# One gate's products moved beside the last delta-rule inverse, with split pools and new durations in the planner

## The chip, the cores and the metric

The kernel runs on one core of a Trainium2 chip. The metric is the device time of one execution in microseconds (us), median of several runs. TensorE (PE) multiplies matrices into PSUM, VectorE (DVE) and ScalarE (ACT) do elementwise work and empty PSUM, GpSimd (POOL) does elementwise work that needs no PSUM, and SyncE (SP) issues nearly all DMAs, in one queue in order.

## The reference

One layer of a hybrid streaming encoder on a sequence of 1024 frames of width 1024, in float32. Cut to what matters here:

```python
h = rmsnorm(x); proj = h @ w_in                     # gdn q,k,v,z,..., gla q,k,v,r,..., gate_a, gate_b
o_a = gated_delta_rule_chunked(q_a, k_a, v_a, ...)  # 8 heads; a unit-triangular solve per chunk, then a scan
o_b = gla_chunked(...)                              # 4 heads
y_a = (rmsnorm(o_a) * silu(z)) @ w_branch_gdn
y_b = (rmsnorm(o_b) * silu(r)) @ w_branch_gla
x = x + (sigmoid(gate_a) * y_a + sigmoid(gate_b) * y_b) @ w_out
x = x + cross_attention(rmsnorm(x), rmsnorm(mem))
x = x + relu(rmsnorm(x) @ w1) ** 2 @ w2
return rmsnorm(x)
```

## The kernel before

**Products.** A float32 operand is split into a high part (`hi`, ACT rounds it, L584) and a rest (`lo`, `raw - hi` on DVE or POOL, L585), and a product is three matmuls of 128x128 by 128x512: hi by hi (L544), hi by lo (L546), lo by hi (L548). Such matmuls are called dense here. Projections use a Strassen-like scheme (`wino`, `gla_dense`) or the plain one (`g_fm`: 2 halves x 8 blocks x 3 = 48 dense matmuls).

**Stages.** `phase0` (norms and memory keys), `phase_gla`, `phase_gdn` (the delta rule), then the merge, the output projection, attention and the MLP. `phase_gdn` works through four pairs of heads. For a pair it makes k, q and v with a convolution (`push_conv`), solves the triangular systems in two parts (a 32-step substitution on DVE and POOL in `gdn_subst`, then `gdn_inverse`), and runs the scan over 8 chunks (`gdn_scan`). The operands of the next pair's convolutions are pushed as generators; `fill(n)` takes n dense matmuls from them, so that dense work is written between the small steps.

**The inverse.** `gdn_inverse` combines 32x32 inverses into 64x64 and 128x128 ones. Per head it has four groups of small matmuls, each needing PSUM results of the one before, copied by ACT or DVE: L1394 (copied at L1395 and L1396), L1403 (copied at L1404 and L1407), L1410 (copied at L1412), L1417 (copied at L1418). Then the scan may begin (L1452). Between the groups stands `fill(nfill)`, with nfill = `GF[6]` = 8.

**The last pair.** Here there is no next pair. The products of gate 5 (`push_gate`: tile `tg`, stored by DMA at L1521) are pushed behind the last convolutions, and before the last inverse

```python
                else:
                    self.drain()
                    ectx.close()
                    wctx.close()
                    ob = self.begin_merge()
```

runs all of them, closes the pools of the stage (`pge`, and `w1` of the weights) and opens those of the merge. `begin_merge` queues the first merge weights (`raw` from `in_w_bgla_dram`) and loads the operands of the first five merge products through staging tiles `e` (from `obd`) into the slots B0a, B0b, A1a, A1b and A0a. The merge's first products (`yb`) multiply weights in tiles `wop` by B0a.

**Order.** The program is traced once, then `Plan` makes an order for each engine: it simulates all instructions with durations from `Op.__init__`, picks by latest start, chooses DVE or POOL for additions that both can do (`flex`), and the order found is fixed with dependencies. Engines take their instructions strictly in that order. A pool may only be written once the instructions on tiles that lay there before are done, and the planner keeps a load behind the closing of every pool that it overlaps. So which matmul stands next to which is set by these costs, pools and the order of the text.

Of the kernel before, what the change touches and what calls it, by code (L numbers as in the profile page):

```python
# [45 lines left out]
LOV = (0, 2, 5)  # L46
GLG, GN = 0, (0, 0, 0, 1)
ZA = "z"
# [34 lines left out]
class Op:  # L83
# [5 lines left out]
    def __init__(self, ins, flex):  # L89
# [27 lines left out]
        if scan:  # L117
            vec = 65 + wide * 2.08
        elif ins.opcode == "StreamTranspose":
            vec = (830 if rough else 90) + wide * 1.042  # L120
        elif ins.opcode == "Reciprocal" or n <= 16 and wide <= 16:
            vec = 82
        pool = {"Memset": 20 + n * 0.875, "TensorScalarAffineSelect": 140 + n * 0.89, "TensorCopy": 140 + n * 0.9}
        self.costs = costs = {"vector": vec, "gpsimd": 245 + n * 1.98 if sums else pool.get(ins.opcode, 100 + n)}
        if sums and n <= 16:
            costs["gpsimd"] = 330 + 160 * n
        if ins.opcode == "DMACopy":
            self.dma, self.cost, self.lat = True, 60, 2600
            self.bytes = n * 4 * outs[0].ap[0][1]
        elif eng == "tensor":  # L130
            m = size(ins_[0])
            if ins.is_transpose:
                self.cost = m * 0.85
            elif ins_[0].dtype == F32R:
                self.cost = m * 0.4427 + (4 if m < HALF else 0)
            else:
                self.cost = max(m, size(ins_[1])) * 1.667 + 8
            self.lat = 205
        elif eng == "scalar":
            self.cost = (60 if psum(ins_[0]) else 95) + n * (1.71 if rough else 0.834) + 90 * min(cols, 1) + 90 * (len(outs) > 1)  # L140
            self.lat, self.own = 140, 130
        else:
            self.port = eng == "gpsimd" or two
            self.place(eng)
# [321 lines left out]
class Layer:  # L466
# [152 lines left out]
    def slot(self, name, shape=(NB, HALF), dt=F32R):  # L619

        pool = self.bp if name[0] == "A" else self.bp2 if name[1] == "0" else self.bp3
        return self.til(pool, (P,) + shape, name, dt, bufs=1)
# [533 lines left out]
    def phase_gla(self):  # L1156
        nc, a = self.nc, self.a
        with ExitStack() as ctx:
# [31 lines left out]
            for h in range(LH):  # L1190
# [32 lines left out]
                if h < LH - 2:  # L1223
                    self.push_gates(sp, 5 + h)
                if h == LH - 2:
                    for i in range(5, 5 + GLG):
                        self.push_gate(i, lambda src: self.wpart(src, [NB, P], nc.vector), sp, "ex", EXB, T)
                self.fill(FG if h == 1 else FE)
# [296 lines left out]
    def phase_gdn(self, wctx):  # L1525

        nc, a = self.nc, self.a
        with ExitStack() as lctx:
            ectx, sctx = ExitStack(), ExitStack()
            sv = self.pool(lctx, "pgv", "left", bufs=2)  # L1530
# [4 lines left out]
            for tag in ("k1", "kdt1", "NT1", "q"):  # L1535
                self.til(sq, [P, T], tag, bufs=2)
            for tag in ("k0", "kdt0", "NT0", "dm", "acc"):
                self.til(sp, [P, T], tag, bufs=2)
            self.til(sq, [P, T], "X", bufs=2)
            self.subTA = self.til(sq, [P, 16, 64], "subTA", bufs=1)  # L1540
# [4 lines left out]
            def push_keys(hs):  # L1545
                par = hs[0] // 2 % 2
                sts = [{"pool": sq if par else sp, "tag": lambda t: f"{t}{par}"} for _ in hs]
                for h, st in zip(hs, sts):
                    st["k"] = self.til(st["pool"], [P, NB, P], st["tag"]("k"), bufs=2)
                    conv(f"k{h}", GH + h, a["w_gdn"][3 * h], lambda acc, st=st: st["k"])  # L1550
                return sts
# [8 lines left out]

            gates = iter(range(5 + GLG, 6))
            getw = lambda src: self.wpart(src, [NB, P])
            last = None
# [3 lines left out]
            for p in range(GH // 2):  # L1567
# [10 lines left out]
                if p < GH // 2 - 1:  # L1578
                    nxt = push_keys((2 * p + 2, 2 * p + 3))
                for _ in range(GN[p]):  # L1580
                    self.push_gate(next(gates), getw, sp)
                if last:
# [12 lines left out]
                self.gdn_queries(sv, sp, sts[1])  # L1595
                self.until(f"v{hs[1]}")
                self.gdn_v(sv, sts[0])
                self.fill(GF[4])
                self.gdn_v(sv, sts[1])
                self.fill(GF[5])  # L1600
                if nxt:
                    self.until(f"k{hs[1] + 2}")
                else:
                    self.drain()
                    ectx.close()
                    wctx.close()
                    ob = self.begin_merge()
                self.gdn_inverse(sts, PF, GF[6])
                if nxt:
                    ns = (2 * p + 2, 2 * p + 3)  # L1610
# [19 lines left out]
    def begin_merge(self):  # L1630

        sp = self.plate = self.pool(self.ctx, "plate", "right")
        self.pad(sp, 32, ([P, HALF], "e", 3), ([P, HALF], "acc", 2), ([P, HALF], "q", 4))
        self.bp2 = self.pool(self.ctx, "big2", "right")
        for n in ("B0a", "B0b"):
            self.slot(n)
        self.wp = self.pool(self.ctx, "w4", "right")
        self.queue_w()
        self.fetch_w()
        ob = {"SL": ("B0a", "B0b", "A1a", "A1b", "A0a", "B1a", "B1b")}  # L1640
        for p in range(5):
            self.load_op(sp, ob, p, lambda p, k: self.obd[p][:, k], range(4), None)
        return ob

    def big3(self, ob):
# [1006 lines left out]
```

## Time and profile before

| | before |
|---|---|
| runs | 2130.86, 2131.04, 2133.01 us; median 2131.04 |
| profiled execution | 2133.65 us, of which the span of instructions is 2131.8 |
| granted TensorE clock, mean | 0.994 |
| busy PE, DVE, ACT, POOL | 2105.4, 1694.6, 1124.6, 198.3 us |
| DMA | 321.7 MB moved, 151 GB/s |

The span is the time from the first to the last instruction. A busy PE is a PE with a matmul in flight, at whatever clock it was granted; "PEclk" gives that clock as a share of full speed. In the rows, "[1.54 <-DVE subTA L1404]" means that the engine stood still for 1.54 us before the instruction, until DVE's write of subTA at L1404 was done.

### The profile page before, as it was taken

To read this page: it belongs to the slowest core of one execution; us is meant where nothing else is said; L and a number is where in the kernel's file an instruction comes from. 1 tells how busy PE (TensorE), PEld (TensorE's weight loads), DVE (VectorE), ACT (ScalarE), POOL (GpSimd) and SP (SyncE) were. 2 spreads that over 40 slices of the span, in tenths; PEclk is the share of its full clock that TensorE was granted. 3 is DMA by queue.
4 is the path that set the end of the run, shared out by engine and by line. 5 is a ranking of instruction groups with operands and counts; after the bars stand their busy time and mean duration, and the time that the engine had idled before them with its cause. 6 is when DMAs were issued, how large, how long until landed. Compare 5 with 4: busy or idle time off the path is not lost.

```text
span 2131.8 us, 31725 instructions
## 1 busy us (share of the span) xinstructions
PE 2105.4 (99%) x11308; PEld 1771.7 (83%) x11308; DVE 1694.6 (79%) x3051; ACT 1124.6 (53%) x2244; POOL 198.3 (9%) x199
## 2 busy tenths in 40 slices
PE   8999999999999999999999999999999999999998
PEld 7898887988888888888888888888888888887877
DVE  7979698879768787777899858788979777577766
ACT  6555454454454747475643446676655556444433
POOL 1102001000001121212010001100200000000001
PEclk9999999999999999999999999999999999999999
DMA  7523333223241030303498653466454556688852
GB/s 279 197 70 111 129 120 114 80 89 120 74 140 60 11 124 12 124 11 118 151 307 299 216 198 112 143 198 220 122 157 141 163 158 183 198 276 267 273 180 91
DMA packets 147040, 321.70 MB, mean 151 GB/s; under 512 B 16056, under 2 KB 19512, under 8 KB 146880
## 3 DMA queue, kind: packets, MB, share of 16 engines
q1 hardware_dynamic: 143984, 315.44, 45.1%
q10 hardware_dynamic: 2896, 4.22, 0.6%
q8 instruction: 89, 1.46, 0.3%
q14 instruction: 71, 0.58, 0.1%
HBM read 223.10 MB, written 96.50 MB: 150 GB/s over the span
## 4 chain that ended last, share of the span: by engine, by line
PE 86%; DVE 6%; DMA 3%; ACT 2%; issue 1%; POOL 0%; SPq 0%; POOLq 0%; DVEq 0%; ACTq 0%
PE pd L544 20%; PE pd L546 20%; PE pd L548 20%; PE ps L544 5%; PE ps L546 5%; PE ps L548 5%; PE ps L616 2%; DMA raw<-in_w_dram 1%; DMA rawa<-ad 1%; DMA e<-ad 1%; PE ps L1452 1%; PE pd L767 1%; PE ps L1459 1%; PE ps L1469 1%; PE ps L1311 1%
## 5 line engine op out<-in xcount | busy, mean ns | idle before, releaser
L584 ACT ACTIVATE wop<-raw 128x512 fp32r<-128x512 f32 (+1 forms) x535 | 355.9, 671 | 527.2 <-PE pd L548 253.8
L585 DVE TENSOR_TENSOR wop<-raw,wop 128x512 fp32r<-128x512 f32 (+1 forms) x512 | 373.6, 734 | 122.7 <-ACT wop L584 115.6
L548 PE MATMUL pd<-A1a,wop 128*128 128x512 f32 x376 | 148.6, 395 | 0.0
L544 PE MATMUL pd<-A1a,wop 128*128 128x512 f32 x376 | 147.1, 392 | 0.0
L546 PE MATMUL pd<-A1b,wop 128*128 128x512 f32 x356 | 139.7, 392 | 0.0
L548 PE MATMUL pd<-t,wop 128*128 128x512 f32 x312 | 124.0, 398 | 0.1
L544 PE MATMUL pd<-t,wop 128*128 128x512 f32 x312 | 121.8, 391 | 2.1 <-ACT wop L584 1.9
L546 PE MATMUL pd<-A1a,wop 128*128 128x512 f32 x312 | 122.8, 394 | 0.2
L546 PE MATMUL pd<-t,wop 128*128 128x512 f32 x312 | 121.7, 390 | 0.0
L544 PE MATMUL pd<-A1b,wop 128*128 128x512 f32 x292 | 115.4, 395 | 0.0
L548 PE MATMUL pd<-A1b,wop 128*128 128x512 f32 x292 | 114.7, 394 | 0.0
L1250 DVE SCALAR_TENSOR_TENSOR acc<-cin,convw,acc 128x1024 f32<-128x1024 f32 x72 | 94.4, 1312 | 15.5 <-ACT acc L1248 14.9
L544 PEld LDWEIGHTS pd<-A1a,wop 128*128 128x128 f32 x376 | 70.7, 188 | 14.3
L548 PEld LDWEIGHTS pd<-A1a,wop 128*128 128x128 f32 x376 | 70.7, 188 | 13.9
L544 PE MATMUL pd<-B0a,wop 128*128 128x512 f32 x196 | 77.1, 394 | 2.5 <-ACT wop L584 2.0
L544 PE MATMUL pd<-A0a,wop 128*128 128x512 f32 x196 | 79.4, 405 | 0.0
L546 PEld LDWEIGHTS pd<-A1b,wop 128*128 128x128 f32 x356 | 66.9, 188 | 13.4 <-DVE A1b L585 0.5
L546 PE MATMUL pd<-A0a,wop 128*128 128x512 f32 x196 | 78.0, 398 | 0.0
L548 PE MATMUL pd<-B0a,wop 128*128 128x512 f32 x196 | 77.4, 395 | 0.0
L548 PE MATMUL pd<-A0a,wop 128*128 128x512 f32 x196 | 77.2, 394 | 0.0
L546 PE MATMUL pd<-A0b,wop 128*128 128x512 f32 x184 | 73.2, 398 | 0.0
L548 PE MATMUL pd<-A0b,wop 128*128 128x512 f32 x184 | 72.6, 395 | 0.0
(660 smaller groups left out, 6025.8 us busy)
## 6 DMA issues: line engine op xcount, KB each, us to landing
raw<-in_w_dram SPq DMA_DIRECT2D x120, 256.0 KB, 4.0
raw<-in_w_dram SPq DMA_DIRECT2D x32, 512.0 KB, 4.4
e<-ad SPq DMA_DIRECT2D x63, 256.0 KB, 4.8
raw<-in_w_gdn_dram SPq DMA_DIRECT2D x24, 512.0 KB, 5.5
ad<-q SPq DMA_DIRECT2D x45, 256.0 KB, 4.6
rawa<-ad SPq DMA_DIRECT2D x42, 256.0 KB, 4.7
A0b<-tgd SPq DMA_DIRECT2D x32, 256.0 KB, 5.1
raw<-in_w_gate_dram SPq DMA_DIRECT2D x15, 512.0 KB, 3.7
```

The source lines that it names most:

```text
L544: nc.tensor.matmul(out, lh, rh, start=first and i == 0, stop=False, skip_group_check=more)
L546: nc.tensor.matmul(out, lh, rl, start=False, stop=False, skip_group_check=more)
L548: nc.tensor.matmul(out, ll, rh, start=False, stop=last and i == n - 1, skip_group_check=more)
L584: nc.scalar.activation(hi, raw, AF.Copy)
L585: (lo_eng or nc.gpsimd).tensor_tensor(lo, raw, hi.bitcast(F32), SUB)
L616: self.nc.tensor.transpose(pt[:, i * P:(i + 1) * P], s, self.ident)
L767: nc.tensor.matmul(pt[:, j * MEM:(j + 1) * MEM], w[k // 4][:, k % 4, js], mf[:, k], start=k == 0, stop=k == NB - 1)
L1250: nc.vector.scalar_tensor_tensor(acc, cin[:, 1 + i:1 + i + T], cw[:, i:i + 1], acc, MUL, ADD)
L1311: nc.tensor.matmul(pt[:, i * P:(i + 1) * P], kc, kc, start=True, stop=True)
L1452: nc.tensor.matmul(py[:, 0:P], st["NT"][:, c, :], zh[h], start=True, stop=True)
L1459: nc.tensor.matmul(pd[h][:, 0:P], st["kd"][:, c, :], dl[h], start=True, stop=True)
L1469: nc.tensor.matmul(po[:, 0:P], st["AT"][:, c, :], dl[h], start=True, stop=True)
```

## The change

Three things change.

1. **Where gate 5 runs.** The pool `pge` loses the tiles k0, kdt0 and NT0 to a pool of their own (`pgk`), which is closed before the last pair. In its room, on the other side, a pool `pgg` holds the gate's weights (`ghi`, `glo`) and results (`tg`). The products of gate 5 are pushed as before, but `drain` now stands behind the last inverse, whose gaps take `GL[2]` = 12 dense matmuls each. The fills in front of the inverse are `GL[0]` and `GL[1]` = 0 (they were 24 and 16), and one `fill(1)` is added. So the pools `pge` and `w1` close before the gate is done.
2. **The merge's pools.** B0a keeps `big2`; B0b moves to a new pool `big4`, opened with the operands 1 to 4 by a new function `begin_ops`, behind the inverse. `begin_merge` loads operand 0 alone.
3. **Durations in the plan.** POOL's copy, selection and additions get dearer, a rough transpose on DVE cheaper for small sizes, and instructions on fewer than 128 partitions 117 ns dearer on ACT and DVE. The planner then fixes another order everywhere. An unused branch for gates in `phase_gla` goes away.

```diff
-GLG, GN = 0, (0, 0, 0, 1)
+GL = (0,0,12)
...
-            vec = (830 if rough else 90) + wide * 1.042
+            vec = 60 + wide * 1.93 if rough else 90 + wide * 1.042
-        pool = {"Memset": 20 + n * 0.875, "TensorScalarAffineSelect": 140 + n * 0.89, "TensorCopy": 140 + n * 0.9}
-        self.costs = costs = {"vector": vec, "gpsimd": 245 + n * 1.98 if sums else pool.get(ins.opcode, 100 + n)}
+        pool = {"Memset": 20 + n * 0.875, "TensorScalarAffineSelect": 140 + n * 1.29, "TensorCopy": 300 + n * 2}
+        self.costs = costs = {"vector": vec, "gpsimd": 320 + n * 1.98 if sums else pool.get(ins.opcode, 100 + n)}
...
+            if outs[0].ap[0][1] < P:
+                self.cost += 117
...
-        pool = self.bp if name[0] == "A" else self.bp2 if name[1] == "0" else self.bp3
+        pool = self.bp if name[0] == "A" else self.bp3 if name[1] == "1" else self.bp2 if name == "B0a" else self.bp4
...
-                for _ in range(GN[p]):
-                    self.push_gate(next(gates), getw, sp)
+                else:
+                    kctx.close()
+                    gp = self.pool(gctx, "pgg", "left")
+                    def getw(src):
+                        raw = self.til(self.wp, [P, NB, P], "raw", bufs=RAWS)
+                        hi, lo = (self.til(gp, [P, NB, P], n, F32R, bufs=1) for n in ("ghi", "glo"))
+                        self.load(raw, src)
+                        self.split(raw, hi, lo)
+                        return hi, lo
+                    self.push_gate(5, getw, gp, "tg", 2)
...
+                if not nxt:
+                    self.fill(1)
                 self.gdn_v(sv, sts[0])
-                self.fill(GF[4])
+                self.fill(GF[4] if nxt else GL[0])
                 self.gdn_v(sv, sts[1])
-                self.fill(GF[5])
+                self.fill(GF[5] if nxt else GL[1])
                 if nxt:
                     self.until(f"k{hs[1] + 2}")
                 else:
-                    self.drain()
                     ectx.close()
                     wctx.close()
                     ob = self.begin_merge()
-                self.gdn_inverse(sts, PF, GF[6])
-                if nxt:
+                self.gdn_inverse(sts, PF, GF[6] if nxt else GL[2])
+                if not nxt:
+                    self.drain()
+                    gctx.close()
+                    self.begin_ops(ob)
+                else:
...
+    def begin_ops(self, ob):
+        self.bp4 = self.pool(self.ctx, "big4", "right")
+        for p in range(1, 5):
+            self.load_op(self.plate, ob, p, lambda p, k: self.obd[p][:, k], range(4), None)
```

Both programs hold the same 10136 matmuls, 1999 instructions on ACT and 977 DMAs. Elementwise work moves: DVE has 3053 instructions before and 3066 now, POOL 204 and 191. Line numbers of the changed file are a little higher: its L548, L550 and L552 are the L544, L546 and L548 of before, L1395, L1404, L1411 and L1418 the L1394, L1403, L1410 and L1417.

TensorE in the last inverse, before: the end of the second head's L1403 and all that follows up to the scan (`ps` is PSUM, `pd` the PSUM of dense products, the other names are those above).

```order
L1403 MATMUL ps_10257<-X_9275,X_9273 32x32
L544 MATMUL pd_10763<-B0a_10092,wop_10713 128x512
L546 MATMUL pd_10763<-B0a_10092,wop_10713 128x512
L1410 MATMUL ps_10288<-subTA_5475,NT_1695_9146 64x64 x8
L1417 MATMUL ps_10299<-NT_1673_9080,X_9275 64x64 x8
L1417 MATMUL ps_10309<-NT_1695_9146,Pm_9176 64x64 x8
L548 MATMUL pd_10763<-B0a_10092,wop_10713 128x512
```

TensorE in the last inverse, now: what stands between the first head's L1404 (32x32) and its L1411 (64x64).

```order
L1404 MATMUL ps_10110<-X_9278,X_9276 32x32
L552 MATMUL pd_10209<-A1b_5351,glo_9985 128x512
L548 MATMUL pd_10209<-A1a_225,ghi_9984 128x512
L550 MATMUL pd_10209<-A1a_225,ghi_9984 128x512
L552 MATMUL pd_10209<-A1a_225,glo_9985 128x512
L548 MATMUL pd_10773<-B0a_10042,wop_10723 128x512
L550 MATMUL pd_10773<-B0a_10042,wop_10723 128x512
L1411 MATMUL ps_10141<-subTA_5478,NT_1673_9083 64x64 x8
```

Before, all 48 products of the gate stand ahead of the inverse, and inside it, up to the last L1417, stand two dense matmuls. Now 37 stand ahead of it, and inside it stand 11 of the gate and 12 of the merge: 7 behind the L1395, 6 as shown, 9 behind the second head's L1404, and one between the two L1418.

SP's queue at the same place, before (`tgd<-tg` stores one half of gate 5).

```order
L1521 DMA tgd_133<-tg_10033 128x512
L504 DMA e_10090<-obd_72 128x512
L504 DMA e_10095<-obd_72 128x512
L504 DMA e_10099<-obd_72 128x512
L1521 DMA tgd_133<-tg_10061 128x512
L504 DMA raw_10082<-in_w_bgla_dram 128x1024
```

SP's queue now.

```order
L508 DMA e_10040<-obd_72 128x512
L508 DMA e_10045<-obd_72 128x512
L508 DMA e_10049<-obd_72 128x512
L1522 DMA tgd_133<-tg_10206 128x512
L508 DMA raw_10032<-in_w_bgla_dram 128x1024
```

The three staging loads moved ahead of the first store of the gate, and the four loads of the merge's first weights stand behind the first store; before they stood behind the second.

DVE's queue around the first copies of the last inverse, before.

```order
L1427 TENSOR_TENSOR v_10019<-ps_10026,vs_9141 128x512
L1396 COPY X_9273<-ps_10177 32x256
L1396 COPY X_9273<-ps_10196 32x256
L1404 COPY subTA_5475<-ps_10215 32x8x32
L1411 COPY NT_1673_9080<-ps_10215 32x8x32
L585 TENSOR_TENSOR B0a_10092<-e_10090,B0a_10092 128x512
```

DVE's queue now.

```order
L1428 TENSOR_TENSOR v_10002<-ps_10009,vs_9144 128x512
L589 TENSOR_TENSOR B0a_10042<-e_10040,B0a_10042 128x512
L589 TENSOR_TENSOR B0a_10042<-e_10045,B0a_10042 128x512
L589 TENSOR_TENSOR B0a_10042<-e_10049,B0a_10042 128x512
L1397 COPY X_9276<-ps_10059 32x256
L1397 COPY X_9276<-ps_10078 32x256
L1405 COPY subTA_5478<-ps_10110 32x8x32
L589 TENSOR_TENSOR wop_10723<-raw_10032,wop_10723 128x512
```

Three rests of B0a moved ahead of the inverse's first copies, and the first rest of a merge weight ahead of L1412.

More of the change, by code (lines that the diff above doesn't have):

```diff
@@ L140, in __init__ @@
             self.cost = (60 if psum(ins_[0]) else 95) + n * (1.71 if rough else 0.834) + 90 * min(cols, 1) + 90 * (len(outs) > 1)
+            if outs[0].ap[0][1] < P:
+                self.cost += 117
             self.lat, self.own = 140, 130
         else:
+            if eng == "vector" and outs[0].ap[0][1] < P:
+                costs["vector"] += 117
             self.port = eng == "gpsimd" or two
@@ L1224, in phase_gla @@
                     self.push_gates(sp, 5 + h)
-                if h == LH - 2:
-                    for i in range(5, 5 + GLG):
-                        self.push_gate(i, lambda src: self.wpart(src, [NB, P], nc.vector), sp, "ex", EXB, T)
                 self.fill(FG if h == 1 else FE)
@@ L1528, in phase_gdn @@
         with ExitStack() as lctx:
-            ectx, sctx = ExitStack(), ExitStack()
+            ectx, sctx, kctx, gctx = (ExitStack() for _ in range(4))
             sv = self.pool(lctx, "pgv", "left", bufs=2)
@@ L1536, in phase_gdn @@
                 self.til(sq, [P, T], tag, bufs=2)
-            for tag in ("k0", "kdt0", "NT0", "dm", "acc"):
+            for tag in ("dm", "acc"):
                 self.til(sp, [P, T], tag, bufs=2)
+            pk = self.pool(kctx, "pgk", "right", bufs=2)
+            for tag in ("k0", "kdt0", "NT0"):
+                self.til(pk, [P, T], tag, bufs=2)
             self.til(sq, [P, T], "X", bufs=2)
@@ L1546, in push_keys @@
                 par = hs[0] // 2 % 2
-                sts = [{"pool": sq if par else sp, "tag": lambda t: f"{t}{par}"} for _ in hs]
+                sts = [{"pool": sq if par else pk, "tag": lambda t: f"{t}{par}"} for _ in hs]
                 for h, st in zip(hs, sts):
@@ L1559, in keys @@
                 return self.gdn_subst(sp, sq, sts)
-            gates = iter(range(5 + GLG, 6))
-            getw = lambda src: self.wpart(src, [NB, P])
             last = None
@@ L1630, in begin_merge @@
     def begin_merge(self):
-        sp = self.plate = self.pool(self.ctx, "plate", "right")
-        self.pad(sp, 32, ([P, HALF], "e", 3), ([P, HALF], "acc", 2), ([P, HALF], "q", 4))
+        self.plate = self.pool(self.ctx, "plate", "right")
+        self.pad(self.plate, 32, ([P, HALF], "e", 3), ([P, HALF], "acc", 2), ([P, HALF], "q", 4))
         self.bp2 = self.pool(self.ctx, "big2", "right")
-        for n in ("B0a", "B0b"):
-            self.slot(n)
+        self.slot("B0a")
         self.wp = self.pool(self.ctx, "w4", "right")
@@ L1640, in begin_merge @@
         ob = {"SL": ("B0a", "B0b", "A1a", "A1b", "A0a", "B1a", "B1b")}
-        for p in range(5):
-            self.load_op(sp, ob, p, lambda p, k: self.obd[p][:, k], range(4), None)
-        return ob
+        self.load_op(self.plate, ob, 0, lambda p, k: self.obd[p][:, k], range(4), None)
+        return ob
+    def begin_ops(self, ob):
+        self.bp4 = self.pool(self.ctx, "big4", "right")
+        for p in range(1, 5):
+            self.load_op(self.plate, ob, p, lambda p, k: self.obd[p][:, k], range(4), None)
     def big3(self, ob):
```

## The prediction

> **What bounds the kernel now.** I read the page's busy times first.
>
> ```profile
> span 2131.8 us, 31725 instructions
> PE 2105.4 (99%) x11308; PEld 1771.7 (83%) x11308; DVE 1694.6 (79%) x3051; ACT 1124.6 (53%) x2244; POOL 198.3 (9%) x199
> ```
>
> PE is in flight for all but 26.4 us of the span, so a change that removes no matmul can win only from those 26.4 us and from time in which PE ran at a lower clock. The table of windows shows where both lie (columns: window and its length, busy time and count of PE, PEld, DVE, ACT, POOL, then PEclk, DMA share, GB/s).
>
> ```profile
> 900.00:1000.00 100.00, 99.90 (x760) 85.83 (x759) 79.28 (x191) 60.16 (x180) 23.36 (x28) 1.00 0.11 38
> 1000.00:1015.00 15.00, 11.47 (x206) 9.24 (x205) 6.20 (x12) 8.43 (x19) 0.10 (x1) 0.78 0.68 233
> 1015.00:1030.00 15.00, 15.00 (x109) 13.63 (x108) 11.06 (x26) 9.06 (x27) 0.00 (x0) 0.76 0.25 84
> 1060.00:1200.00 140.00, 139.46 (x620) 115.05 (x619) 138.36 (x227) 60.24 (x104) 13.02 (x6) 1.00 0.85 291
> ```
>
> Only around 1000 to 1030 is the clock low for long. That is the last inverse. PE's timeline there shows two waits, and finer windows the clock:
>
> ```profile
> 1004.19 1.81 PE L1394 MATMUL ps<-X,NT 32*32 32x32 f32 x58
> ...
> 1008.43 1.91 PE L1410 MATMUL ps<-subTA,NT 64*64 64x64 f32 x16 [1.54 <-DVE subTA L1404]
> ...
> 1013.30 0.80 PE L544 MATMUL pd<-B0a,wop 128*128 128x512 f32 x1 [1.96 <-ACT wop L584]
> ```
>
> ```profile
> 1006.00:1007.00 1.00, 0.85 (x52) 0.58 (x45) 0.15 (x1) 0.95 (x3) 0.00 (x0) 1.00 1.06 250
> 1008.40:1010.00 1.60, 1.57 (x15) 1.60 (x16) 0.41 (x1) 1.05 (x3) 0.00 (x0) 0.52 0.88 335
> 1021.00:1022.00 1.00, 1.00 (x5) 0.81 (x4) 0.39 (x1) 0.89 (x2) 0.00 (x0) 0.50 0.00 0
> 1022.00:1023.00 1.00, 1.00 (x7) 0.91 (x7) 0.46 (x2) 0.68 (x2) 0.00 (x0) 0.94 0.00 0
> ```
>
> So PE stands 1.54 us for a copy and 1.96 us for the first merge weight, and from about 1008.4 to 1022.06 runs at half clock, though from 1013.30 on it is never idle. The three inverses of the other pairs, which have dense work between their groups, show neither. They and the last one side by side, each from its first L1394 to the end of its last L1417; the last row is the rest of the half clock:
>
> ```profile
> 698.17:711.06 12.89, 12.89 (x248) 10.67 (x247) 8.28 (x11) 9.08 (x18) 0.10 (x1) 1.00 0.11 38
> 803.71:816.51 12.80, 12.80 (x247) 10.66 (x246) 8.28 (x11) 9.08 (x18) 0.10 (x1) 1.00 0.13 40
> 909.13:921.96 12.83, 12.83 (x247) 10.66 (x247) 8.27 (x11) 9.08 (x18) 0.10 (x1) 1.00 0.12 41
> 1004.19:1019.39 15.20, 11.67 (x227) 10.40 (x226) 6.99 (x13) 9.81 (x21) 0.06 (x1) 0.64 0.60 209
> 1019.39:1022.06 2.67, 2.67 (x9) 2.28 (x9) 1.89 (x3) 0.89 (x2) 0.00 (x0) 0.50 0.00 0
> ```
>
> **The inverse, the main term.** An inverse has 224 small matmuls (64 + 96 + 32 + 32, as the profile counts them). The counts say that the earlier ones hold 22 dense matmuls besides and the last one 2 (the odd one or two of a window belong to its edges). The price of a dense matmul is the step between starts:
>
> ```profile
> 992.41 0.39 PE L546 MATMUL pd<-A0a,wop 128*128 128x512 f32 x1
> ...
> 1000.14 0.39 PE L548 MATMUL pd<-A1a,wop 128*128 128x512 f32 x1
> ```
>
> 34 steps in 7.73 us, 0.227 each. An earlier inverse without its dense matmuls is 12.8 - 22 x 0.227 = 7.8 us. The last would take 7.8 + 2 x 0.227 = 8.3 at full clock and takes 15.20: 6.9 us lost. The 2.67 us behind it at half clock lose 1.3 more. Together 8.2 us, of which 3.5 are the waits and 4.7 the clock. An upper end: halving all busy time from 1008.4 to 1022.06 (13.7 - 1.96 = 11.7, so 5.9) and adding 3.5 gives 9.4; but the shortest matmuls need not double with the clock, so I stay with 8.2, which compares equal work.
>
> In the new order 23 dense matmuls stand inside the last inverse, as many as the 22 of the others. None is new work: 11 are the gate's, from ahead of the inverse, 12 the merge's, from behind it. If they can run when their turn comes, the last inverse becomes a fourth like the three: about 13 us at full clock.
>
> **Can they run?** The gate's 11 can: its weights are split before the inverse begins. The merge's need B0a and the first `wop`. Before, the queue of SP and the landing times were:
>
> ```profile
> 998.48 0.32 SPq L1521 DMA_DIRECT2D tgd<-tg  x1
> 998.84 1.40 SPq L504 DMA_DIRECT2D e<-obd  x3
> 1004.92 0.32 SPq L1521 DMA_DIRECT2D tgd<-tg  x1
> 1005.28 2.78 SPq L504 DMA_DIRECT2D raw<-in_w_bgla_dram  x4
> ```
>
> ```profile
> raw<-in_w_bgla_dram SPq DMA_DIRECT2D x4, 512.0 KB, 6.2
> e<-obd SPq DMA_DIRECT2D x4, 256.0 KB, 3.8
> ```
>
> The weights wait behind the gate's second store. Now they stand behind the first, whose half of the gate is still ahead of the inverse, so they go at about 998.8 and land, 6.2 us on, at 1005. With 11 gate products taken out, the inverse starts at 1004.19 - 2.5 = 1001.7. PE needs the first weight after L1394 (2 us), seven dense (1.6), half of L1403 (0.7) and four dense (0.9), so at 1006.9 or later: 1005 and 0.6 for ACT's split leaves about 1 us to spare. Those four loads pass one store of the gate, 0.3 us of issue; the store passed by them has no reader before the merge. DVE now has three splits of B0a (0.69 each) ahead of L1396, whose result PE needs 3.4 us after L1394 starts; their `e` loads moved ahead of the first store, so they should land by 1002.6 at the latest (998.8 + 3.8), and I price the delay at 0 to 1 us and take 0. ACT has the same three ahead of its first copies, at the same price. On POOL the memset that opens the merge's pool now stands ahead of its two copies to subTA; it waits for old users of `w1`, now the last convolution's matmuls in place of the gate's, so it is free before the inverse, cost 0.
>
> **What comes after.** The merge is the next place. In 1060 to 1200 DVE is busy for 138.36 of 140 us, so a PE that arrives 8 us early could find DVE late. DVE gets two more instructions there (the split of A0a, and L1507), 1.4 us at the mean of this row:
>
> ```profile
> L585 DVE TENSOR_TENSOR wop<-raw,wop 128x512 fp32r<-128x512 f32 x48 | 32.8, 687 | 0.1
> L1507 POOL TENSOR_TENSOR v<-AT,AT 128x512 f32<-128x512 f32 x1 | 5.3, 5291 | 0.8 <-DVE AT L1497 0.8
> ```
>
> On the other side, up to the scan's first state copy (L1462), DVE has by the new order done 15 elementwise instructions of the merge where it had done 8: 7 x 0.687 = 4.8 us of its backlog is gone before the scan. Against that stand the 10 dense matmuls (2.3 us) by which PE is ahead in work. DVE's margin to PE thus changes by 4.8 - 1.4 - 2.3 = +1.1 us: the gain passes through, cost 0, ends -1 and +1.4. The second row shows what POOL is worth there: 5.3 us for a sum like those DVE does in 0.69. [...]
>
> **The new durations** move 13 more instructions to DVE in all and change the order everywhere. PE's other waits are few:
>
> ```profile
> PE pd L544 <- ACT wop L584: 6.7, 5, 2.2
> PE ps L1410 <- DVE subTA L1404: 1.5, 1, 1.5
> PE pd L548 <- DVE wlo L585: 1.5, 2, 1.1
> PE ps L1111 <- DVE v L1121: 1.0, 1, 1.0
> ```
>
> The best the new order can do elsewhere is to remove what is left of these, 4.7 + 1.5 + 1.0 = 7.2 us. The worst is bounded by a row of the MLP, where one wait of 2.2 us was followed by a short fall of the clock:
>
> ```profile
> 1940.00:1944.00 4.00, 1.77 (x7) 1.18 (x7) 2.63 (x5) 1.73 (x4) 0.00 (x0) 0.96 0.97 297
> 1944.00:1948.00 4.00, 4.00 (x12) 3.12 (x11) 4.00 (x8) 2.63 (x6) 0.00 (x0) 0.61 0.81 257
> ```
>
> 2.2 + 0.39 x 4 = 3.8 us for one such event. One gone or one more is about as likely, so I take 0, with ends -4 and +4.
>
> **The sum.** 2133.65 - 8.2 = 2125.4 us for the profiled execution. That execution is 2.6 us above the median of the runs, so against 2131.04 the forecast is 2122.8 us, 0.39% faster.
>
> [...]
>
> **The rivals.**
> - *A wait stays in the inverse.* If `e` or the first weight lands 2 us later than I put it, or DVE's three splits delay L1396, PE stands once more amid small matmuls. With a wait of 1.5 to 2 us the clock goes to half again, as at 1008.4. The gain is then 8.2 - 1.8 - 4.7 = 1.7 us: about 2129.3. For it speak the DMA share of 1.06 at 1006, against it the spare 1 us and the 11 gate products, which need no load. Chance 0.12.
> - *The merge's DVE takes the gain.* If DVE cannot use the earlier start, PE waits before 1200 until DVE has done its work, which ends no sooner than before and has 1.4 us more: 2131.04 + 1.4 = 2132.4. It decides if DVE has done fewer than 8.2 / 0.687 = 12 instructions more by the time that PE leaves the merge. Against it speaks the margin worked out above. Chance 0.07.
> - *The change doesn't do what it says.* If the weights still go out only with the gate's second store (now after the gate's last product inside the inverse, at about 1007), they land at 1013, PE waits 6 us at the first B0a product, and the time is as before, 2131. The order speaks against it. Chance 0.03.
> - *Slower: the reordered MLP.* Its second product lives on transfers (DMA share 0.97 in the row above) and already had one wait at 1941. With a changed order of loads there, each weight that comes late costs 3.8 us. Three use up the gain (8.2 - 11.4), and with four the time is 2131.04 - 8.2 + 15.2 = 2138. No row shows loads that late more than once. Chance 0.05.
>
> **How the numbers follow.** The likeliest case has 0.73, with its own range from 2118.5 (9.4 and 3 of the other waits gone) to 2126.8 (4 us lost elsewhere). A change of 0.2%, 4.3 us, is about what a measurement of this kernel can tell from none. All of the likeliest case but its upper edge is faster by more; the first three rivals, 0.22, are mostly within 0.2%. So faster 0.74, same 0.20, slower 0.06. The range from 2118.5 to 2130 leaves out the slow rival, the second, and some edges.
>
> **What would show it.** Right: in the last inverse no wait of PE over 0.5 us, PEclk 1.00 in every window from its first L1394 to the scan, its length about 13 us with some 23 dense matmuls, the first weights issued about 6 us before the gate's second store; in the merge DVE still at about 98% and PE waiting under 1 us. Wrong: a half clock anywhere in the 25 us around the inverse, PE waits in the merge of more than 3 us in sum, or new waits of 2 us in the MLP.

## The result and the profile after

The changed kernel takes 2116.85 us (median of 6 runs, 2115.67 to 2119.44), the kernel before beside it 2131.39 (6 runs, 2130.60 to 2133.01). The ratio is 0.9932, 95% interval 0.9920 to 0.9945: 14.5 us less. The forecast was 2122.8, 8.2 us less, and the lower end of its range 2118.5. The profiled execution after took 2116.06 us; it lies 17.6 us below the profiled one of before, which was 2.3 us above the median of its own runs.

The head of the page after:

```profile
span 2114.3 us, 31740 instructions
PE 2097.1 (99%) x11308; PEld 1766.9 (84%) x11308; DVE 1692.1 (80%) x3064; ACT 1126.3 (53%) x2244; POOL 172.8 (8%) x186
```

PE was idle for 17.2 us in place of 26.4. That is 9.2 us; the other 8.3 of the 17.5 us by which the span is shorter are less busy time. The half clock of before is part of that, since a dense matmul is in flight for 0.80 us at half clock (at 1013.30 in the kernel before) and for 0.39 at full. The windows of the last inverse (its first L1395 to the end of its last L1418), of the scan behind it and of the merge, in the same columns as before:

```profile
997.86:1011.18 13.32, 13.32 (x249) 10.92 (x248) 11.19 (x21) 10.27 (x21) 0.00 (x0) 1.00 0.53 205
...
1015.00:1030.00 15.00, 15.00 (x106) 13.44 (x104) 13.52 (x36) 12.97 (x44) 0.00 (x0) 1.00 0.40 140
...
1060.00:1200.00 140.00, 139.81 (x615) 114.95 (x614) 133.16 (x219) 60.71 (x105) 4.54 (x3) 1.00 0.81 284
```

The inverse holds 23 dense matmuls, is never idle and keeps the full clock, as does the scan. PE's waits, longest sums first (us in total, how many, the longest):

```profile
PE pd L552 <- DVE wlo L589: 1.5, 2, 1.1
PE ps L723 <- POOL ident masks.py:199: 1.5, 1, 1.5
PE pd L771 <- ACT mf L706: 1.5, 1, 1.5
PE pd L548 <- DVE u L1882: 1.2, 1, 1.2
PE pd L550 <- DVE wlo L589: 0.8, 1, 0.8
PE pd L548 <- ACT wop L588: 0.7, 1, 0.7
```

The two waits of the inverse are gone, but so are three others: the 1.0 us at L1111 in the GLA stage, the 2.2 us for a weight at 1943.6 in the MLP, and 1.36 us for a load in the first 10 us. The prediction's list of waits has the first two and takes neither as gone; the third is not in its list.

To see where the time went I priced every matmul at the median step from the one before it, by the shapes of the two, and call the rest of PE's time "lost" (small steps between shapes, waits and half clock; a table of my own, not a view). The stages are cut at 100, 350, 900, 1050 and 1850 us of priced work, so that the same work is compared. All kernels of the experiments are in it, each by its profiled execution:

| lost, us | start | GLA | delta rule | last inverse, scan | merge to MLP | rest of MLP | median time |
|---|---|---|---|---|---|---|---|
| before | 18.7 | 12.0 | 25.6 | 13.7 | 5.9 | 7.1 | 2131.4 |
| after | 16.6 | 9.7 | 25.0 | 7.2 | 5.2 | 2.4 | 2116.9 |
| e1, durations only | 17.3 | 9.6 | 25.1 | 15.5 | 4.4 | 7.4 | 2130.4 |
| e2, move only | 18.2 | 12.0 | 25.8 | 9.1 | 6.5 | 6.9 | 2126.8 |
| e3, gate before | 16.8 | 9.6 | 25.1 | 9.0 | 5.5 | 0.4 | 2117.5 |
| e8, useless work | 18.4 | 12.0 | 25.6 | 8.1 | 8.5 | 4.7 | 2130.9 |
| e9, before with MLP of after | 17.5 | 12.0 | 25.6 | 15.0 | 6.1 | 2.0 | 2128.1 |
| e10, after with MLP of before | 17.5 | 9.7 | 25.1 | 7.3 | 5.3 | 6.3 | 2121.4 |
| e5, POOL's prices | 17.1 | 10.2 | 26.2 | 14.8 | 4.6 | 2.4 | 2125.4, one run |
| e4, narrow instructions | 19.5 | 10.8 | 25.9 | 14.8 | 6.5 | 10.3 | 2138.0, one run |
| e12, before, slower loads | 17.4 | 11.1 | 26.5 | 14.0 | 5.6 | 7.3 | 2135.4 |
| e13, after, slower loads | 18.4 | 11.7 | 25.2 | 7.2 | 4.9 | 4.8 | 2121.5 |

From before to after: 2.1 us in the start, 2.3 in GLA, 0.6 in the delta rule, 6.5 in the last inverse and its scan, 0.7 behind it, 4.7 in the MLP. What two executions of one order differ by shows in before and e9, equal up to the MLP: 1.2 us in the start (where before waits 1.36 us for a load) and 1.3 in the inverse; and in after and e3, equal in the MLP: 2.0 us there. Smaller differences in a column say little, since each row is one execution.

### The profile page after: what moved, and what is told of

It is laid out like the page before. It is cut to its first block, busy times and chain, and to the rows that moved or that the text cites. A ratio compares the mean times of both kernels' runs of the same rounds, so it can differ in the third digit from the quotient of the medians.

```text
span 2114.3 us, 31740 instructions
## 1 busy us (share of the span) xinstructions
PE 2097.1 (99%) x11308; PEld 1766.9 (84%) x11308; DVE 1692.1 (80%) x3064; ACT 1126.3 (53%) x2244; POOL 172.8 (8%) x186
## 4 chain that ended last, share of the span: by engine, by line
PE 95%; DVE 2%; DMA 1%; issue 1%; ACT 1%; DVEq 0%; POOLq 0%; ACTq 0%; SPq 0%
PE pd L550 22%; PE pd L548 22%; PE pd L552 22%; PE ps L548 6%; PE ps L550 6%; PE ps L552 6%; PE ps L620 2%; PE pd L771 1%; PE ps L1453 1%; PE ps L1470 1%; PE ps L1460 1%; PE ps L1312 1%; PE ps L1326 1%; PE ps L1115 1%; PE ps L1443 1%
## 5 line engine op out<-in xcount | busy, mean ns | idle before, releaser
L552 PE MATMUL pd<-A1a,wop 128*128 128x512 f32 x372 | 147.1, 395 | 0.0
L548 PE MATMUL pd<-A1a,wop 128*128 128x512 f32 x372 | 146.5, 394 | 0.0
L550 PE MATMUL pd<-A1b,wop 128*128 128x512 f32 x352 | 138.6, 394 | 0.0
L552 PE MATMUL pd<-t,wop 128*128 128x512 f32 x312 | 123.7, 397 | 0.0
L548 PE MATMUL pd<-t,wop 128*128 128x512 f32 x312 | 122.1, 391 | 1.4 <-DVE u L1882 1.2
L550 PE MATMUL pd<-t,wop 128*128 128x512 f32 x312 | 121.6, 390 | 0.0
L550 PE MATMUL pd<-A1a,wop 128*128 128x512 f32 x308 | 121.4, 394 | 0.1
L552 PE MATMUL pd<-A1b,wop 128*128 128x512 f32 x288 | 113.6, 394 | 0.0
L548 PE MATMUL pd<-A1b,wop 128*128 128x512 f32 x288 | 112.8, 392 | 0.0
L548 PEld LDWEIGHTS pd<-A1a,wop 128*128 128x128 f32 x372 | 70.0, 188 | 13.8 <-ACT A1a L588 0.3
L552 PEld LDWEIGHTS pd<-A1a,wop 128*128 128x128 f32 x372 | 69.9, 188 | 13.8
L548 PE MATMUL pd<-A0a,wop 128*128 128x512 f32 x192 | 77.6, 404 | 0.0
L550 PEld LDWEIGHTS pd<-A1b,wop 128*128 128x128 f32 x352 | 66.1, 188 | 13.3
L550 PE MATMUL pd<-A0a,wop 128*128 128x512 f32 x192 | 76.8, 400 | 0.0
L552 PE MATMUL pd<-B0a,wop 128*128 128x512 f32 x196 | 76.6, 391 | 0.0
L548 PE MATMUL pd<-B0a,wop 128*128 128x512 f32 x196 | 76.4, 390 | 0.0
L552 PE MATMUL pd<-A0a,wop 128*128 128x512 f32 x192 | 75.8, 395 | 0.0
L550 PE MATMUL pd<-A0b,wop 128*128 128x512 f32 x180 | 71.0, 395 | 0.0
L552 PE MATMUL pd<-A0b,wop 128*128 128x512 f32 x180 | 70.9, 394 | 0.0
```

The lines of the kernel that those rows point to most:

```text
L548: nc.tensor.matmul(out, lh, rh, start=first and i == 0, stop=False, skip_group_check=more)
L550: nc.tensor.matmul(out, lh, rl, start=False, stop=False, skip_group_check=more)
L552: nc.tensor.matmul(out, ll, rh, start=False, stop=last and i == n - 1, skip_group_check=more)
```

## The experiments

### e1: the durations alone

The kernel before with point 3 of the change only (all the new durations).

> The kernel before with the new durations alone; gate and pools as before. Up to the last inverse its order is that of the changed kernel, instruction for instruction; the last inverse has only 2 to 3 dense matmuls in it, as before; in the MLP the order of the loads agrees with neither. Theory A (each stretch keeps the time that its own order gives; the durations are worth only the waits of the early stages): the wait at the GLA scan (L1111, 1.0 us) and its neighbours go, about 2 us; the last inverse keeps its 15 us and about 13.6 us of half clock; the MLP has a wait of its own or not (0 or 5 us). So 2131.4 - 2 = 2129.4, or 2124.5 if the MLP is free of waits. Theory B (the durations gave all of the gain that I had not forecast, 14.5 - 8.2 = 6.3 us, the MLP's among it): 2125.1, with an MLP without waits. Theory C (the whole gain comes from the inverse and what follows on it): 2131.4, no change.

2130.44 us (11 runs) beside 2131.72 (21 runs); ratio 0.9995 (0.9986 to 1.0003). The last inverse waits and slows as before (PE's timeline, then the window of its half clock, then PE's timeline in the MLP):

```profile
1004.87 1.94 PE L1414 MATMUL ps<-subTA,NT 64*64 64x64 f32 x16 [1.54 <-DVE subTA L1408]
...
1009.24 0.79 PE L548 MATMUL pd<-B0a,wop 128*128 128x512 f32 x1 [1.44 <-ACT wop L588]
```

```profile
1003.44:1020.51 17.07, 14.20 (x129) 12.08 (x130) 8.46 (x16) 9.59 (x20) 1.27 (x1) 0.50 0.45 164
```

```profile
1947.88 0.50 PE L548 MATMUL pd<-B1a,wop 128*128 128x512 f32 x1 [3.66 <-ACT wop L588]
```

The early stages are as short as in the changed kernel (GLA 9.6). The inverse lost 1.8 us more than before, by a longer half clock, and the MLP has one wait of 3.66 us in place of those of 2.23 and 1.49. Theory A holds place by place; theory B, that the durations gave the surplus, falls. The total alone could not tell A from theory C, no change, since the interval reaches 1; the early stages of the table speak against C.

The half clock did not come from the wait of 1.54 us. It began at 1003.43, 0.1 us into that wait (1004.87 less 1.54 is 1003.33). In the 3.41 us before it PE was in flight almost without a break, at first with the last dense matmuls and then with 32x32 ones alone:

```profile
1000.02:1003.43 3.41, 3.28 (x115) 2.61 (x114) 0.43 (x1) 2.51 (x6) 0.10 (x1) 1.00 0.42 122
1003.43:1006.84 3.41, 1.97 (x22) 1.88 (x25) 1.48 (x4) 3.03 (x7) 0.00 (x0) 0.50 0.97 356
```

So in e1 the fall came behind a stretch of mostly small matmuls with 0.13 us of idle time.

### e2: the move alone

The changed kernel with the old prices (third hunk taken back).

> The changed kernel with the old durations: the gate's move and the split pools alone. The last inverse holds 15 dense matmuls, all of the gate, and none of the merge; up to it the order is that of the kernel before, and in the MLP nearly that of the changed kernel. Theory A (the MLP's gain came with the move, through the order that it leaves there): inverse 7 and MLP 5 us less, 2131.4 - 12 = 2119.4, no wait of 2 us in the MLP, L1111's wait of 1.0 us still there. Theory B (the MLP's gain came from the durations): 2131.4 - 7 = 2124.4, and the MLP's wait of 2.2 us is there. In both no half clock at the inverse; if there is one, the 12 merge products inside the inverse are needed and 15 dense do not do.

2126.78 us (5 runs); ratio 0.9966 (0.9953 to 0.9978), above the times of both theories. The stretch from the end of the third scan to the end of the last, in before, in after and here:

```profile
966.11:1052.58 86.47, 82.94 (x646) 71.98 (x646) 66.96 (x152) 51.29 (x154) 16.71 (x12) 0.92 0.37 127
```

```profile
963.05:1042.00 78.95, 78.95 (x647) 67.58 (x647) 67.81 (x157) 51.03 (x153) 10.22 (x12) 1.00 0.41 144
```

```profile
965.90:1043.20 77.30, 76.41 (x634) 65.28 (x634) 65.16 (x143) 49.33 (x148) 16.16 (x15) 1.00 0.40 136
```

All hold the same 452 other matmuls (one of each count only reaches into the window), so 193, 194 and 181 dense ones. Less 0.2273 each, the price of the forecast, they take 42.6, 34.9 and 36.2 us: the inverse and its scan give 7.7 us in the changed kernel and 6.4 with the gate's products alone, at full clock (13 of them stand in the inverse, not the 15 expected). Of theory A's MLP half came true: the wait at 1943 is gone, but another place has one (PE's timeline), with 3.4 us of half clock behind it.

```profile
2042.82 0.61 PE L544 MATMUL pd<-t,wop 128*128 128x512 f32 x1 [2.99 <-DVE u L1878]
```

The changed kernel waits 1.19 us at that place. So neither half of the change has the MLP's gain: 7.4 and 6.9 us lost there in e1 and e2, 7.1 before, 2.4 with both. The parts do not add: 1.3 + 4.9 us, and 14.5 together. What in both halves together leads the planner to its better order of the MLP stays open.

### e3: the gate ahead of the inverse again

```diff
                 else:
+                    self.drain()
                     ectx.close()
                     wctx.close()
                     ob = self.begin_merge()
```

> The changed kernel with one line more: all products of the gate are run before the last inverse, as in the kernel before, while pools and durations are the new ones. Everywhere but in the last inverse and the scan behind it the order is that of the changed kernel. The inverse holds 20 dense matmuls, all of the merge. Theory A (what counts is that some dense work is ready when its turn comes, whose does not matter; the split pools let the first merge weights go out with the gate's first store): no half clock, at most 1 us of waiting for the first weight, 2116.9 to 2118. Theory B (the gate's products are needed because the merge's weights land too late): a wait of 1.5 us or more in the inverse, half clock, +5 to +8 us: 2122 to 2125.

2117.49 us (5 runs); ratio 0.9928 (0.9915 to 0.9940), as the changed kernel. The inverse, with 20 dense matmuls, all of the merge:

```profile
1000.37:1013.62 13.25, 13.15 (x245) 10.12 (x244) 10.10 (x17) 11.93 (x25) 1.28 (x1) 1.00 0.45 152
```

Theory A holds: whose products stand there does not matter. The stretch takes 1.9 us more than in the changed kernel (81.29 less 196 x 0.227 = 36.7), and the same order of the MLP lost 2.0 us less in this execution, so the two are equal in sum. The merge's products alone do it here, as the gate's alone do in e2. Here the merge's weights left SP's queue at 994.98, right behind the gate's first store; whether they must leave so early is not shown, as no run with the new pools holds them back.

### e8: useless work in the kernel before

```diff
     def fill(self, n):
+        if n < 0:
...
+            pt = self.psd()
+            x = self.hk(0, 0)[0]
+            for _ in range(-n):
+                self.nc.tensor.matmul(pt, x[:, :P], x, start=True, stop=True)
+            return
...
-                self.gdn_inverse(sts, PF, GF[6])
+                self.gdn_inverse(sts, PF, GF[6] if nxt else -8)
```

It fills the first three gaps of the last inverse.

> The kernel before, with 24 added dense matmuls in the last inverse (8 behind L1394, 8 behind each head's L1403) that write a PSUM tile nobody reads: useless work of 24 x 0.227 = 5.4 us, as much as the other inverses hold of useful work. Up to the inverse the order is that of before; behind it that of the MLP differs, so the time of the whole is read with care (0 or 5 us) and the inverse in the profile. Theory A (the loss of the last inverse is waits and the half clock that they bring, and dense work in the gaps removes both): PEclk 1.00 through the inverse and the scan, the inverse 13 us long in place of 15.2, half clock gone; the stretch ends 2 to 3 us earlier than before though it holds 5.4 us more of work; in all 2128.5 to 2129.5, or 2124 if the MLP is free of waits too. Theory B (the clock falls because of the many small matmuls, whatever stands between them): half clock as before, 2131.4 + 5.4 x 2 = 2142.

2130.90 us (10 runs); ratio 0.9993 (0.9983 to 1.0002): 5.4 us more of work cost nothing. The inverse and its stretch:

```profile
965.71:1050.09 84.38, 84.22 (x667) 71.12 (x667) 67.81 (x150) 52.11 (x153) 18.57 (x13) 1.00 0.39 132
1003.66:1017.61 13.95, 13.95 (x250) 11.14 (x249) 7.96 (x15) 11.08 (x23) 0.07 (x1) 1.00 0.66 228
```

Theory A holds for the stage: no wait and PEclk 1.00. Less its 214 dense matmuls the stretch takes 35.7 us, 6.9 less than before. It is 2.1 us shorter than before though it holds 21 dense matmuls, 4.8 us, more. In the sum of the run this is not to be seen, since the order behind it is another one (merge +2.6, MLP -2.4). The loss of the inverse thus comes from the empty gaps: dense matmuls that nobody needs remove it here, as the gate's do in e2 and the merge's in e3 (PEclk 1.00 in each).

### e9 and e10: the MLP's order alone

These two put one kernel's order of the MLP into the other. The order of every engine from the start of `phase_mlp` on is taken from the other kernel (the instructions are the same in both; `MLP` holds the other kernel's order and its choice of DVE or POOL):

```diff
-            made = p.args[0]
+            made = _mlp_order(p.args[0])
...
+    for q, s in zip(made[0], order):
+        s = iter([CUT + i for i in s])
+        new = [i if i < CUT else next(s, None) for i in q]
+        queues.append([i for i in new if i is not None] + list(s))
+    return queues, made[1][:CALLS] + engines, made[2]
```

> The kernel before, in which the orders of all engines in the MLP (every instruction from the start of phase_mlp, and which of them POOL does) are those that the changed kernel has there; all ahead of the MLP is as before. Theory A (the 4.9 us of the MLP come from the order alone, which the planner came to by chance with the new costs and pools together): no wait of 2 us near 1944 and no half clock there, at most the 1.2 us behind u, so 2131.7 - 4.9 = 2126.8. Theory B (the order is right only for the times at which the changed kernel gets there; put behind another merge it waits elsewhere): within 1.5 us of before, 2130 to 2133.

2128.14 us (11 runs); ratio 0.9982 (0.9973 to 0.9991), 3.5 us less than before (1.9 to 5.8). The windows around the old wait, and what is left later:

```profile
1940.00:1944.00 4.00, 4.00 (x19) 3.31 (x18) 3.19 (x6) 2.19 (x5) 0.00 (x0) 1.00 1.00 341
1944.00:1948.00 4.00, 4.00 (x19) 3.33 (x18) 3.19 (x6) 1.51 (x4) 0.00 (x0) 1.00 0.80 273
```

```profile
2046.10 0.50 PE L544 MATMUL pd<-t,wop 128*128 128x512 f32 x1 [1.07 <-DVE u L1861]
```

> The changed kernel in which the orders of all engines in the MLP are those of the kernel before. Theory A (order alone): the wait of 2.2 us for wop, the half clock of 3.4 us behind it and the 1.5 us at the end come back, 2116.9 + 4.9 = 2121.8, and that is near the 2122.8 which I had forecast without a gain in the MLP. Theory B (the early arrival of the changed kernel is what keeps the MLP free of waits): 2116.9 to 2118.

2121.41 us (5 runs); ratio to before 0.9956 (0.9942 to 0.9970), 4.6 us more than the changed kernel. The old wait is back, and half clock behind it:

```profile
1932.38 0.80 PE L548 MATMUL pd<-B0b,wop 128*128 128x512 f32 x1 [2.70 <-ACT wop L588]
...
2038.63 0.47 PE L548 MATMUL pd<-t,wop 128*128 128x512 f32 x1 [1.06 <-DVE u L1882]
```

```profile
1932.21:1935.60 3.39, 3.22 (x8) 2.58 (x9) 3.24 (x6) 2.33 (x6) 0.00 (x0) 0.50 0.84 263
```

Theory A in both directions: the MLP's part of the gain, 3.5 and 4.6 us by the times, 5.1 and 3.9 by the table, is a matter of its order, whatever runs ahead of it. PE's own order is not what differs: by the traces its matmuls run in the same order in e9 as in before, to the last one, and in e10 as in after. The orders that feed it differ, those of ACT, DVE, POOL and SP; which of them counts was not tried. Without it the changed kernel stands at 2121.4, 1.4 us from the forecast.

### e5 and e4: one price each

e5 is the kernel before with POOL's new prices alone, e4 with the 117 ns for narrow instructions alone.

> The kernel before with the dearer prices of POOL alone (copy, selection, sums). In the GLA stage the kernel before has DVE's L1264 at 2.62 us where it takes 1.21 alone, while POOL does the same sum beside it, and PE waits 1.0 us at L1111. Theory A (the early gain of 2.3 us is POOL's sums gone to DVE): L1264 is no longer on POOL, no wait at L1111, the stretch from 100 to 350 us as short as with all the new durations. Theory B (the price of narrow instructions did it): the wait at L1111 is there as before. The time as a whole says little, since the MLP has its own order.

> The kernel before with the 117 ns for instructions on fewer than 128 partitions alone. Theory A (POOL's prices did the early gain): the sum L1264 still goes to POOL, the wait at L1111 of 1.0 us stays. Theory B: the wait goes. The last inverse as before, 2 to 3 dense matmuls in it and 13.6 us of half clock, in both.

The wait at L1111 in the kernel before, read on PE, DVE and POOL:

```profile
329.15 0.67 PE L1111 MATMUL ps<-v,ex 128*128 128x256 f32 x2 [0.99 <-DVE v L1121]
```

```profile
326.05 2.62 DVE L1264 TENSOR_TENSOR ex<-ex,tm 128x1024 f32<-128x1024 f32 x1
328.60 0.41 DVE L1121 COPY v<-ps 128x256 f32<-128x256 f32 x1
```

```profile
325.68 1.91 POOL L1264 TENSOR_TENSOR ex<-ex,tm 128x1024 f32<-128x1024 f32 x1
```

DVE's product takes 2.62 us and ends 1.08 us behind POOL's, which ends at 327.59; the copy that PE needs stands behind it. In after DVE does these products alone, in 1.22 us:

```profile
323.89 1.22 DVE L1265 TENSOR_TENSOR ex<-ex,tm 128x1024 f32<-128x1024 f32 x1
```

The wait is gone in e5 (one run, 2125.35), but not as I expected: one L1264 is still on POOL (1.91 us from 321.83 on), but beside it DVE now has a small instruction, which takes 1.82 us there and 0.16 at 319.04, at a moment when PE has other work.

```profile
321.94 1.82 DVE L1267 TENSOR_TENSOR kf<-gge,tm 128x8 f32<-128x8 f32 x1
```

It is gone in e4 too (one run, 2138.02), where theory A expected it to stay: no L1264 is on POOL in this stretch, though POOL's prices are the old ones. What the kernels without the wait share is that the two engines no longer do this product at the same time, and either price alone brings that about; no run changes this one thing by itself. e4 loses 10.3 us in the MLP, by two waits each with half clock behind it:

```profile
1951.20 0.50 PE L548 MATMUL pd<-B1a,wop 128*128 128x512 f32 x1 [3.25 <-ACT wop L588]
...
2054.55 0.79 PE L548 MATMUL pd<-t,wop 128*128 128x512 f32 x1 [2.36 <-DVE u L1865]
```

### e12 and e13: loads that land later in the plan

```diff
-            self.dma, self.cost, self.lat = True, 60, 2600
+            self.dma, self.cost, self.lat = True, 60, 3600
```

> The kernel before with one number of the plan changed: a DMA lands 3.6 us after its issue in place of 2.6 (the profile shows 4.5 to 4.7 us for the loads e and rawa, which the plan puts at 2.6 + 0.9). The whole order changes. Theory A (the MLP's waits come from loads that land later than the plan believes, behind which the weights' sums wait in DVE's queue): no wait of 2 us in the MLP, 2131.6 - 5 = 2126.6. Theory B (each new order is a new draw, whatever the number): an MLP with waits between 0 and 6 us, 2125 to 2132. The last inverse keeps its half clock in both.

> The changed kernel with the same one number: loads land 1 us later in the plan. The last inverse has 22 dense matmuls, the gate's and the merge's, nearly as in the changed kernel. Theory A: the last wait of the MLP (1.2 us behind u) goes too, 2115.7, or a little better where other loads are waited for. Theory B (a new draw): 2115 to 2123.

e12: 2135.38 us (11 runs; the profiled execution, at 2132.84, is the lowest of them), ratio 1.0018 (1.0009 to 1.0027). e13: 2121.46 us (5 runs), ratio 0.9953 (0.9940 to 0.9965). Both are slower than the kernels that they come from, and both have waits of 2 us for weights in the MLP. Theory A falls: a plan with the loads nearer to their real time does not order the MLP better. Each order is a new draw, with waits that the changed number does not foretell (theory B; e12 lies even above its range). The last inverse of e13, with 22 dense matmuls, is free of half clock, that of e12, with none, is not.

## Why the forecast was right in sign and wrong in size

**The main term held.** It said 8.2 us; the stretch gave 7.7 when equal work is taken off, and 6.5 through the table. How long the half clock of an empty inverse lasts is itself a draw: with the order of before, e9 lost 1.3 us more there. In the changed kernel there was no wait over 0.5 us, the inverse took 13.3 us with 23 dense matmuls, and PEclk was 1.00 up to the scan's end. The weights went out at 995.03, behind the gate's first store, 9.5 us ahead of the second:

```profile
994.66 0.32 SPq L1522 DMA_DIRECT2D tgd<-tg  x1
995.03 1.88 SPq L508 DMA_DIRECT2D raw<-in_w_bgla_dram  x4
...
1004.49 0.32 SPq L1522 DMA_DIRECT2D tgd<-tg  x1
```

ACT's first split of a weight and the first product with it:

```profile
1001.94 0.63 ACT L588 ACTIVATE wop<-raw 128x512 fp32r<-128x512 f32 x1
```

```profile
1003.25 0.40 PE L548 MATMUL pd<-B0a,wop 128*128 128x512 f32 x1
```

The split ends at 1002.57, 0.7 us ahead of its use; the forecast said 1. That dense work removes the half clock was right too: six kernels with 13 to 24 dense matmuls in the last inverse (after, e2, e3, e8, e10, e13) have no half clock there, six with 0 to 3 (before, e1, e4, e5, e9, e12) have 10.2 to 17.1 us of it.

**The step that failed is "The new durations": "One gone or one more is about as likely, so I take 0, with ends -4 and +4."** It was worth 2.9 us in GLA and the delta rule and, with the move, 4.7 us in the MLP. Three faults in it:
- I counted PE's waits only: 1.0 us at L1111. The table's method, cut finer, gives 1.6 us of the 2.3 around that place (300 to 320 us of priced work). The row that told more stood in the trace, DVE's L1264 at 2.62 us beside POOL's; I had read a long sum of POOL at L1507 (5.3 us) in the merge and did not look elsewhere for such a pair.
- The gains lie in several places, each with its own order. I let the ends of one event (4 us) stand for all of them. The best case of 7.2 us was in the text, but the range took 3 of it.
- For the MLP a mean of 0 was fair: the nine orders lost 2.4 to 10.3 us, half of them within 4.7 and 7.3, and the kernel before 7.1. But such a draw can win 4.7 us, and the lower end had 3 us for this and the early stages together.

2122.8 less 2.9 and 4.7, plus the 0.5 by which the main term was smaller, gives 2115.7; measured 2116.85. That it comes so near is in part luck: the start and the merge are left out, and one order of the MLP lost 2.0 us more in one execution than in another. e10, where the MLP's part is taken out, is at 2121.4.

**The profiled execution against the median.** For 1.2 of the 2.6 us that were subtracted the runs show a reason: up to the MLP e9 has the order of before and lost 17.5 us in the start, not 18.7. There the profile of before held 1.36 us of waiting for a load and a spell of half clock, which the others mostly lack; that of e8 has both too, and it is the slowest of e8's ten runs.

**The merge.** DVE is busy for 133.16 us of the 140, not the 98% that I named, and PE waits 0.2 us. POOL went from 13.02 to 4.54 us there. DVE's 5.2 us less are fewer instructions in the window (219 in place of 227), not faster ones: the row that the prediction gave with 687 ns has 684 now.

```profile
L589 DVE TENSOR_TENSOR wop<-raw,wop 128x512 fp32r<-128x512 f32 x47 | 32.1, 684 | 1.6 <-ACT wop L588 1.5
```

That the sum L1507 left POOL made nothing on DVE faster: in the kernel before, while POOL took its 5.29 us from 1074.98 on, DVE's instructions kept their 0.69 us.

```profile
1076.62 0.69 DVE L1759 TENSOR_TENSOR raw<-raw,raw 128x512 f32<-128x512 f32 x1
```

**The rivals.** A wait in the inverse: none came, at 0.7 us to spare. The merge's DVE taking the gain: no. A change without effect: no. The reordered MLP with three or four late weights: no kernel has more than two waits over 2 us there, but e4, with two, lost 10.3 us in the MLP and is 6.4 us slower than before. The mechanism is real, and its draw here went the other way.

**The half clock.** The prediction's first rival took the idle time of 1.54 us as what brings it. In e1 it began 0.1 us into such a wait. The term keeps its size, since dense work removed the wait and the fall alike: with it the inverses of e2, e3 and e8 stood still for 0.55, 0.10 and 0.00 us and kept PEclk 1.00. The spell among small matmuls lasted 13.64 us in before and 17.07 us in e1. The forecast was worked out from the spell as measured in the kernel before, and that is what there was to win.

## What to carry to other kernels

Where a planner orders everything, a change moves all later stages too: price the stages ahead of and behind the edit as separate draws, add their ends to the edit's own, and look up what the present order loses in each, since a stage that loses much has more to win. To tell the edit from the draw, put one stage's order of one kernel into the other, both ways (e9 and e10). Dense work in the gaps of the chain of small matmuls kept PEclk at 1.00 here whatever it computed (13 to 24 dense matmuls in e2, e3 and e8), so any product that is ready is worth a try.

## What the runs showed of the hardware

**The half clock lasted 3.41 us or a few times that.** Behind a wait among dense matmuls it lasted 3.40 us (before), in the empty inverses 10.22 (e12), 13.64 (before) and 17.07 us (e1): 1, 3, 4 and 5 steps of 3.41 us. Windows on two spells in the kernel before, and on that of e12:

```profile
1008.47:1022.11 13.64, 11.68 (x122) 10.28 (x123) 7.60 (x13) 6.76 (x14) 0.00 (x0) 0.50 0.48 175
1943.72:1947.12 3.40, 3.40 (x9) 2.66 (x10) 3.40 (x6) 2.03 (x5) 0.00 (x0) 0.50 0.79 268
```

```profile
1006.81:1017.03 10.22, 9.69 (x117) 8.93 (x116) 6.58 (x12) 5.68 (x12) 0.00 (x0) 0.50 0.60 224
```

The two spells of before begin 935.25 us apart. The longer one is 13.653 us long in the trace's clock records, a fourth of it 3.4133 us, and 935.25 us are 274.0 such steps. A third spell (8.36 to 11.77) begins 1000.10 us ahead of the longer one, 293.0 steps. So the steps of before lie on one grid. The same order drew 13.65 us of half clock in before and 17.07 in e9.

In e1 the fall among small matmuls came behind a step with 0.13 us without a matmul in flight (above). Among dense ones it came behind longer idle times. Cut into the steps of their own traces, the waits of all twelve kernels in dense stretches give six steps with 1.96 to 2.99 us without a matmul in flight, each followed by half clock, and no fall behind a step with 1.69 us or less. The nearest on both sides, e4 (a wait of 2.36 us, with 1.96 of it in this step), then e12 (1.69 us, all in one step) and e13 (a wait of 2.01 us, of which the step holds 1.54):

```profile
2050.75:2054.16 3.41, 1.45 (x7) 0.87 (x5) 3.41 (x4) 1.89 (x3) 3.41 (x3) 1.00 0.86 289
2054.16:2057.57 3.41, 3.02 (x7) 2.44 (x8) 3.41 (x7) 0.63 (x1) 1.52 (x2) 0.50 0.69 220
```

```profile
1945.46:1948.87 3.41, 1.72 (x8) 1.12 (x7) 2.62 (x5) 1.26 (x4) 0.00 (x0) 1.00 0.85 308
1948.87:1952.28 3.41, 3.41 (x17) 2.80 (x16) 3.27 (x6) 1.75 (x5) 0.00 (x0) 1.00 0.75 256
```

```profile
1935.87:1939.28 3.41, 1.87 (x9) 1.22 (x7) 1.99 (x3) 0.84 (x2) 0.00 (x0) 1.00 1.03 372
1939.28:1942.70 3.42, 2.95 (x13) 2.46 (x14) 2.97 (x5) 2.36 (x5) 0.00 (x0) 1.00 0.95 323
```

No dense step stood still for between 1.69 and 1.96 us, so what follows on such a step is not shown.

**DVE's products beside POOL's.** In the GLA stage of before POOL's product ended at 327.59 and DVE's, 2.62 us long from 326.05 on and 1.22 alone, ended 1.1 us later. In e5 POOL's ended at 323.74 and DVE's small one, 1.82 us long from 321.94 on and 0.16 elsewhere, at 323.76. In the merge of before DVE's instructions beside POOL's L1507 kept their 0.69 us. What sets these cases apart is not shown.
